# The last two expert places combined on TensorE, and the context branch moved into the expert stage

## The chip, the cores and the metric

The kernel runs on one core of a Trainium2 chip. The metric is the device time of one execution in microseconds (us), the median of several runs. Places in the trace are given in us from the start of the span.

## The reference, cut to what matters

Two transformer blocks follow one another on 512 tokens of 1024 numbers, all in fp32. The first block ends in a mixture of experts: each token goes to 2 of 32 experts. The second block takes the normed sum, and also a second, short sequence, the context (256 tokens), of which only one small state is needed.

```python
# first block, after its mixer (TOP_K = 2, N_EXPERTS = 32)
def expert_block(args):
    xb, e = args
    hid = jax.nn.silu(xb @ w_gate[e]) * (xb @ w_up[e])
    return hid @ w_down[e]
y = jnp.sum(y_buf[dest].reshape(T, TOP_K, D) * weights[..., None], axis=1)
x = x + y
# second block
h_lat = _rms_norm(x, norm_mix) * (1.0 + sc1) + sh1
h_ctx = _rms_norm(ctx, norm_mix) * (1.0 + csc1) + csh1
... = jnp.split(h_lat @ w_in, ...)
... k_c, v_c, ..., gf_c, gb_c = jnp.split(h_ctx @ w_in, ...)
s_f = _gla_final_state(kh_c, vh_c, lgf_c)                # k, v and log gates of the context
s_b = _gla_final_state(_rev(kh_c), _rev(vh_c), _rev(lgb_c))
o_l = _gla_bidir(qh_l, kh_l, vh_l, lgf_l, lgb_l, s_f, s_b)   # starts from these two states
```

`_log_gate` is a product with a narrow matrix, a second one, and a log-sigmoid; `_gla_final_state` sums k, times an exponential of a running sum of the log gates, times v.

## The kernel before, in words

**Expert stage.** The rows of the 512 tokens are sorted by expert into 34 slots of 64 rows. The kernel visits them as 32 "places": places 1 to 24 have one slot of 64 rows, 25 and 26 have two (128 rows), 27 to 32 one. A place loads 12 chunks of 512 KB of its expert's weights (eight for up and gate, four for down) and multiplies each in plain fp32, two products of 512 columns (`products` in `expert_block`). SyncE (SP) issues all chunk loads in order into a ring of tiles called "raw"; the ring has 25 tiles (`wraw`, `mr`, `nr`, `whi`, `wlo`, `xr`), 19 after place 13. A load waits until TensorE is done with the tile's last user. The order of TensorE's instructions is written by hand: `ORDER = "uuutssgududssududu"` says, for each place, when an up/gate chunk of this place (u), a transposition or down chunk of the place before (t, d), a step of gathering rows for a later place (g) or a step of side work (s) comes. The side work from place 13 on is `spectrum` (filters of the second block); in place 31 it is `context_hidden`.

**What a place leaves.** y of a place (64 x 1024) goes from PSUM by a DVE copy (L891) and an ACT copy to a tile, and by a DMA to a buffer in HBM (`ybuf`, `g.Y`). So y of place k is copied while place k+1 runs. Beside the 34 slots `ybuf` has 15 blocks for a rare overflow; they are filled with zeros early on (`zz`). A loop `For_i` after the last place handles overflow blocks; with this input it runs no time, but its bound is loaded from SBUF into each engine's registers, and the engines pass its branch.

**After the last place.** `context` runs on TensorE (with weights split into two fp32r halves and three products for one, `dense_nat`), while POOL issues eight indirect gathers `yk<-ybuf` (128 rows of 4 KB each, L971). On DVE eight scalar-tensor-tensor operations (L977) add them, weighted, to the residual x, which was loaded again from HBM after the last chunk (`load_x`, L247). Then come squares, a square root by eleven small DVE operations (`rsqrt`), the scaled rows `xn`, and `mixer2` transposes them (`hidden_T`, L1237) and starts its big products.

Of the kernel before, what the change touches and what calls it, by code (L numbers as in the profile page):

```python
# [24 lines left out]
SPEC = 13  # L25


ORDER = "uuutssgududssududu"

# [220 lines left out]
def mixer1(g, mp):  # L250
# [95 lines left out]
    for kt in range(8):  # L346
# [311 lines left out]
def routing(g, first):  # L658
# [131 lines left out]
    g.sloti = g.b2c.tile([128, 2, 4], I32, name="sloti")  # L790
    V.tensor_copy(g.sloti, g.slot)
# [59 lines left out]
def expert_block(g, pool, x, e, store, queue=None):  # L851


    nc, A = g.nc, g.A
    n = x.shape[2]
    w = A["l_moe"][e] if isinstance(e, int) else A["l_moe"][ds(e, 1)].rearrange("o p a c -> (o p) a c")
# [8 lines left out]
    def products(ps, lhs, c, first, last):  # L865
        raw = ring(g, "raw", [128, 2, 512], F32)
        nc.sync.dma_start(raw.rearrange("p a b -> p (a b)"), w[:, c, :])
        for i in range(2):
            nc.tensor.matmul(ps[i], lhs, raw[:, i, :], start=first, stop=last)  # L869
# [20 lines left out]
    y = g.yg.tile([128, 1024], F32, name="y", tag="y", bufs=2)[0:n]  # L890
    nc.vector.tensor_copy(y[:, 0:512], pd[0])  # L891
    nc.scalar.activation(y[:, 512:1024], pd[1], AF.Copy)  # L892
    (queue or nc.gpsimd).dma_start(store, y)
# [3 lines left out]
def moe(g, pool, xg):  # L897
# [8 lines left out]
    place, last, side = 0, None, iter(())  # L906
    with g.tc.manual_schedule(engines={mybir.EngineType.PE}):
        for i, (b0, nb, double) in enumerate(groups):
            steps, nxt = rows(i + 1) if i + 1 < len(groups) else (iter(()), None)
            if i == 7:  # L910
                context_norm(g, pool)
            next(steps, None)
            for b in range(0, nb, 2 if double else 1):
                e = place
                if place >= DBL:
                    e = nc.values_load(g.eoi[0:1, 32 + place:33 + place], engines=[eng], min_val=0, max_val=31)
                place += 1
                r0, n = (b0 + b) * 64, 128 if double else 64
                block = expert_block(g, pool, xg[0][:, :, b * 64:b * 64 + n], e, g.Y[r0:r0 + n, :],
                                     queue=nc.scalar if place == 32 else None)  # L920
                if place == SPEC:

                    g.rings["raw"] = [r for r in g.rings["raw"] if r[0] is not g.resid and r[1] != "nr"]
# [1041 lines left out]
```

## Time and profile before

| | us |
|---|---|
| Median of 3 runs (lowest, highest) | 1560.48 (1560.05, 1561.49) |
| Profiled execution, whole | 1556.2 |
| Its span, first to last instruction | 1554.2 |
| TensorE (PE) busy in it | 1457.9 (94 %) |
| VectorE (DVE) busy | 797.5 (51 %) |
| ScalarE (ACT) busy | 525.9 (34 %) |
| GpSimd (POOL) busy | 128.2 (8 %) |
| First and last y copy of the expert stage (L891) | 370.5, 864.8 |
| Mean granted TensorE clock | 0.976 |

A busy PE is one with a product in flight, which can still be slow or wait for its weights; so the stage has to be read by what PE waits for and by the distance of the y copies. The profiled execution took 4.3 us less than the median of the runs; sums are made within it.

### The profile page before, as it was taken

How to read it: one execution, taken by the hardware profiler on the slowest of the kernel's cores; microseconds unless marked ns; L12 is line 12 of the kernel's file. 1: busy time of each engine (PE TensorE's matmuls, PEld its weight loads, DVE VectorE, ACT ScalarE, POOL GpSimd, SP SyncE). 2: the span in 40 equal slices, each digit the busy share in tenths (PEclk: the TensorE clock that was granted, in tenths of full speed). 3: DMA queues.
4: the chain of work that ended last, by engine and by line, in shares of the span. 5: the costliest groups of instructions: out<-in, count | busy, mean ns of one | idle time of the engine just before them, and what ended most of it. 6: DMA issues, size and time to landing. Idle time of an engine off the chain costs nothing. (4 is left out here: it accounts for less than half of the span.)

```text
span 1554.2 us, 19403 instructions
## 1 busy us (share of the span) xinstructions
PE 1457.9 (94%) x7024; PEld 989.4 (64%) x7024; DVE 797.5 (51%) x1496; ACT 525.9 (34%) x859; POOL 128.2 (8%) x119
## 2 busy tenths in 40 slices
PE   7999999959999889899999689999999999999997
PEld 6776777844443234444444458887787888888886
DVE  6888858681111340312202494789868652344344
ACT  5444545321111242421112353333435442134331
POOL 1111000030000010110100220000301000000010
PEclk9999999979999999899999799999999999999999
DMA  8442261768999999999999835336522522222321
GB/s 282 128 156 89 87 185 54 241 258 329 410 410 410 381 409 411 381 368 409 373 385 410 309 119 163 97 109 202 162 97 98 200 88 89 95 95 96 101 89 55
DMA packets 123450, 343.10 MB, mean 221 GB/s; under 512 B 11823, under 2 KB 14866, under 8 KB 123352
## 3 DMA queue, kind: packets, MB, share of 16 engines
q1 hardware_dynamic: 115576, 320.15, 57.2%
q0 software_dynamic: 5248, 17.10, 2.8%
q10 hardware_dynamic: 2528, 4.59, 1.0%
q8 instruction: 56, 0.92, 0.3%
q14 instruction: 42, 0.34, 0.1%
HBM read 322.69 MB, written 19.14 MB: 220 GB/s over the span
## 5 line engine op out<-in xcount | busy, mean ns | idle before, releaser
L151 DVE TENSOR_TENSOR wlo<-wraw,whi 128x1024 fp32r<-128x1024 f32 (+2 forms) x136 | 163.9, 1205 | 207.2 <-ACT whi L150 206.2
L150 ACT ACTIVATE whi<-wraw 128x1024 fp32r<-128x1024 f32 (+1 forms) x142 | 146.9, 1034 | 341.3 <-PE acc L157 189.8
L891 DVE COPY y<-acc 64x512 f32<-64x512 f32 (+1 forms) x32 | 21.8, 682 | 234.2 <-PE acc L869 234.2
L869 PE MATMUL acc<-mr,xg 128*64 128x512 f32 (+1 forms) x488 | 127.5, 600 | 4.8 <-DMA mr<-in_l_moe 4.7
L156 PE MATMUL acc<-h3hi,whi 128*128 128x512 f32 (+1 forms) x272 | 102.8, 379 | 1.1 <-ACT h3hi L1263 1.1
L157 PE MATMUL acc<-h3hi,wlo 128*128 128x512 f32 (+1 forms) x272 | 102.4, 377 | 0.0
L158 PE MATMUL acc<-h3lo,whi 128*128 128x512 f32 (+1 forms) x272 | 102.0, 378 | 0.1
L158 PE MATMUL acc<-wlo,mh 128*128 128x512 f32 x224 | 88.8, 397 | 0.0
L157 PE MATMUL acc<-whi,ml 128*128 128x512 f32 x224 | 88.7, 396 | 0.0
L156 PE MATMUL acc<-whi,mh 128*128 128x512 f32 x224 | 88.7, 396 | 0.0
L892 ACT ACTIVATE y<-acc 64x512 f32<-64x512 f32 (+1 forms) x32 | 19.0, 593 | 192.4 <-DVE y L891 170.9
L869 PEld LDWEIGHTS acc<-mr,xg 128*64 128x64 f32 (+1 forms) x488 | 34.9, 139 | 77.2 <-issue 53.0
L1046 DVE SCALAR_TENSOR_TENSOR adac<-wraw,sc,adac 128x512 f32<-128x512 f32 x100 | 80.3, 810 | 6.6 <-POOL adac L1042 3.2
L869 PE MATMUL acc<-wraw,xg 128*64 128x512 f32 (+1 forms) x276 | 71.6, 602 | 1.8 <-DMA wraw<-in_l_moe 1.8
L156 PE MATMUL acc<-whi,xh 128*128 128x512 f32 x160 | 64.4, 402 | 8.3 <-ACT whi L150 8.3
L869 PE MATMUL acc<-mr,hT 128*64 128x512 f32 (+1 forms) x252 | 69.8, 597 | 1.1 <-DMA mr<-in_l_moe 1.1
L157 PE MATMUL acc<-whi,xl 128*128 128x512 f32 x160 | 64.0, 400 | 0.0
L158 PE MATMUL acc<-wlo,xh 128*128 128x512 f32 x160 | 63.8, 401 | 0.0
L156 PEld LDWEIGHTS acc<-h3hi,whi 128*128 128x128 f32 x272 | 51.2, 188 | 10.5 <-ACT h3hi L1263 1.3
L846 PE MATMUL pgx<-G,hh 128*128 128x256 f32 (+1 forms) x288 | 53.7, 311 | 4.5 <-DVE G L827 4.5
L158 PEld LDWEIGHTS acc<-h3lo,whi 128*128 128x128 f32 x272 | 50.9, 188 | 9.7 <-DVE h3lo L1265 0.3
L157 PEld LDWEIGHTS acc<-h3hi,wlo 128*128 128x128 f32 x272 | 51.2, 188 | 9.2
(704 smaller groups left out, 2987.8 us busy)
## 6 DMA issues: line engine op xcount, KB each, us to landing
mr<-in_l_moe SPq DMA_DIRECT2D x185, 512.0 KB, 10.7
wraw<-in_l_moe SPq DMA_DIRECT2D x94, 512.0 KB, 10.1
wraw<-in_w_mlp SPq DMA_DIRECT2D x64, 512.0 KB, 3.9
wraw<-in_w_in SPq DMA_DIRECT2D x56, 512.0 KB, 4.0
wraw<-in_w_ada SPq DMA_DIRECT2D x48, 512.0 KB, 3.7
whi<-in_l_moe SPq DMA_DIRECT2D x36, 512.0 KB, 10.3
wlo<-in_l_moe SPq DMA_DIRECT2D x35, 512.0 KB, 10.2
xr<-in_l_moe SPq DMA_DIRECT2D x20, 512.0 KB, 10.7
```

What stands on the lines that cost most here:

```text
L150: nc.scalar.activation(hi[:, :nk, :ncol], raw[:, :nk, :ncol], AF.Copy)
L151: eng.tensor_tensor(lo[:, :nk, :ncol], raw[:, :nk, :ncol], hi[:, :nk, :ncol], op=OP.subtract)
L156: g.nc.tensor.matmul(ps, ah, bh, start=start, stop=False)
L157: g.nc.tensor.matmul(ps, al, bh, start=False, stop=False)
L158: g.nc.tensor.matmul(ps, ah, bl, start=False, stop=stop)
L846: nc.tensor.matmul(pg[:, :n], src[:, tt, ks], G[:, tt, :n], start=i + tt == 0, stop=i == 1 and tt == 3)
L869: nc.tensor.matmul(ps[i], lhs, raw[:, i, :], start=first, stop=last)
L891: nc.vector.tensor_copy(y[:, 0:512], pd[0])
L892: nc.scalar.activation(y[:, 512:1024], pd[1], AF.Copy)
L1046: nc.vector.scalar_tensor_tensor(acc[v], raw[:, k, :], s, acc[v], op0=OP.mult, op1=OP.add)
```

## The change

1. The zero fill of `ybuf` goes, and `ybuf` has only the first 32 slots.
2. The context branch is made inside the expert stage: its norm beside place 5, the rest as side work of places 9 to 12, as plain fp32 products from weights loaded into six tiles of the ring. Its state is copied to `S0` there. `context_hidden` in place 31 and `context` after the loop go.
3. The residual x is loaded again before place 31's chunks, no longer after the last chunk.
4. Places 31 and 32 keep their y in SBUF (a `spare` tile) and follow an order of their own, `LAST`. A one-hot matrix times the weights (`slot_weights`) is made as side work in place 31.
5. After place 30 the eight gathers are issued, into ring tiles, and eight DVE operations (L1047) add them to x.
6. After the loop `add_rows` adds places 31 and 32: eight fp32 products of 128 x 128 by 512 columns, and eight DVE additions from PSUM. Squares are on ACT, and there are two root chains (three rows of tiles, then one).
7. An overflow block would add to x in the loop itself.

```diff
-SPEC = 13
+SPEC, CTX = 13, 2
+LAST = "uuutsuddddssuuuu"
...
-    zz = mp.tile([64, 1024], F32, name="zz", tag="p", bufs=4)
-    nc.gpsimd.memset(zz, 0.0)
-    nc.sync.dma_start(g.Y[64 * NST:64 * (NST + NMAX), :].rearrange("(b p) c -> p b c", p=64),
-                      zz[:, None, :].to_broadcast([64, NMAX, 1024]))
...
-            if i == 7:
+            if i == CTX - 1:
                 context_norm(g, pool)
+            if i == CTX:
+                side = context(g, pool)
...
-                if place == 31:
-                    for _ in side:
-                        pass
-                    side = context_hidden(g, pool)
...
+        load_x(g, g.xs)
+        spare = [g.moe.tile([128, 2, 512], F32, name="spare", tag="nr", bufs=g.nn) for _ in range(2)]
+        keep = spare[0].rearrange("p a b -> p (a b)")
+        side = last_slots(g, pool, groups[-1][0], spare[1])
+        for b in range(2):
+            block = expert_block(g, pool, xg[0][:, :, b * 64:b * 64 + 64], chunks(), keep[b * 64:b * 64 + 64], keep=True)
+            run(LAST, block)
+            if b == 0:
+                gathered(g)
...
-    load_x(g, g.xs)
-
-    context_load(g)
...
+    more_blocks(g, pool, nmore)
+    add_rows(g, keep, g.wl)
+    squares(g)
...
+def gathered(g):
     nc = g.nc
+    y = {}
     for tt in range(4):
         for k in range(2):
+            y[tt, k] = ring(g, "raw", [128, 2, 512], F32).rearrange("p a b -> p (a b)")
+            nc.gpsimd.indirect_dma_start(out=y[tt, k], out_offset=None, in_=g.Y,
                                          in_offset=bass.IndirectOffsetOnAxis(ap=g.sloti[:, k, tt:tt + 1], axis=0))
+    for tt in range(4):
+        for k in range(2):
+            x = g.x[:, tt, :]
+            nc.vector.scalar_tensor_tensor(x, y[tt, k], g.wy[:, k, tt:tt + 1], x, op0=OP.mult, op1=OP.add)
+
+
+def add_rows(g, y, w):
+
+    for tt in range(4):
+        for h in (slice(0, 512), slice(512, 1024)):
+            ps = g.ps.tile([128, 512], F32, name="pc", tag="acc" if h.start else "t", bufs=4)
+            g.nc.tensor.matmul(ps, w[:, tt * 128:tt * 128 + 128], y[:, h], start=True, stop=True)
+            x = g.x[:, tt, h]
+            g.nc.vector.tensor_tensor(x, x, ps, op=OP.add)
...
+    def half(c0, out):
+
+        ps = g.ps.tile([128, 2, 256], F32, name="pkv", tag="t", bufs=4)
+        raw = []
+        for c in (0, 4):
+            raw.append(ring(g, "raw", [128, 2, 512], F32).rearrange("p a b -> p (a b)").rearrange("p (a b) -> p a b", a=4))
+            nc.sync.dma_start(raw[-1], A["w_in_2"][0][c * 128:c * 128 + 512, c0:c0 + 256].rearrange("(a p) c -> p a c", p=128))
+        for tt in range(2):
+            for k in range(8):
+                nc.tensor.matmul(ps[:, tt], h[:, k, tt * 128:tt * 128 + 128], raw[k // 4][:, k % 4], start=k == 0, stop=k == 7)
+            if tt == 0:
+                yield
+        nc.scalar.activation(out, ps, AF.Copy)
         yield
```

TensorE in the middle of places 9 to 12, as it stands now (L879 is a chunk's product, L891 the transpositions of gu, L1439 the context's narrow product, L1398 the gates, L1456 its k and v):

```order
L879 MATMUL acc<-whi,hT 64x512 x2
L1439 MATMUL pgr<-hc,wg2f 32x256 x8
L1398 MATMUL pz<-gk,gr 128x512 x2
L879 MATMUL acc<-xr,xg 64x512 x2
...
L891 MATMUL pth<-identf,gu 128x64 x4
L1456 MATMUL pkv<-mr,hc 128x256 x16
L840 MATMUL pgx<-G,hh 128x256 x4
...
L879 MATMUL acc<-mr,hT 64x512 x2
L1456 MATMUL pkv<-mr,hc 128x256 x16
L879 MATMUL acc<-mr,xg 64x512 x2
```

The context's products stand between chunk products, where before only chunk products stood.

SP at the end of the chunk loads, as it stands now with its waits (L855 is a chunk load; the last five are the last up/gate chunk and the four down chunks of place 32; `DMASW` are the gathers, `PE` and `DVE` the tile's last user):

```order
L855 DMA mr_6607<-in_l_moe 128x1024 [waits DMAHW2_49,PE_49]
L855 ISA
L855 DMA whi_6611<-in_l_moe 128x1024 [waits DMAHW3_49,DMASW5_49,DVE_49]
...
L855 DMA wlo_6627<-in_l_moe 128x1024 [waits DMAHW4_49,DMASW6_49,DVE_49]
...
L855 DMA wraw_6639<-in_l_moe 128x1024 [waits DMAHW7_49,DMASW1_49,DVE_49]
L139 DMA wraw_7073<-in_w_in_2 128x2x512 [waits DMAHW0_49,DMASW2_49,DVE_49]
...
L1134 DMA wraw_7114<-in_w_ada_2 128x2x512 [waits DMAHW3_49,PE_49]
L989 COMPARE_AND_BRANCH
```

The last five chunks now wait for a gather and for the DVE addition that reads it; four loads for `mixer2` stand ahead of the loop's branch.

DVE at the end of the stage, before (L891 y copy, L877 gate times up, L977 the additions of gathered rows, L1365 the context's k times its exponential):

```order
L891 COPY y<-acc 64x512
L877 TENSOR_TENSOR gu<-acc,gu 64x512
L891 COPY y<-acc 64x512
L151 TENSOR_TENSOR wlo<-wraw,whi 128x2x256
L948 TENSOR_LOAD eoi
...
L977 SCALAR_TENSOR_TENSOR xb<-yk,wk,xb 128x1024 x2
L1365 TENSOR_TENSOR kw<-s4c,kn 128x2x4x64
L977 SCALAR_TENSOR_TENSOR xb<-yk,wk,xb 128x1024
L1365 TENSOR_TENSOR kw<-s4c,kn 128x2x4x64
L980 SCALAR_TENSOR_TENSOR yk,css<-xa 128x1024 x2
```

and now (L901 y copy, L887 gate times up, L1047 the additions of gathered rows, L1057 those from `add_rows`):

```order
L901 COPY y<-acc 64x512
L887 TENSOR_TENSOR gu<-acc,gu 64x512
L1047 SCALAR_TENSOR_TENSOR xa<-whi,wy,xa 128x1024
...
L1047 SCALAR_TENSOR_TENSOR xb<-wraw,wy,xb 128x1024 x4
L901 COPY spare<-acc 64x512
L887 TENSOR_TENSOR gu<-acc,gu 64x512
L901 COPY spare<-acc 64x512
L941 TENSOR_LOAD eoi
...
L1057 TENSOR_TENSOR xa<-xa,pc 128x512 x4
L1057 TENSOR_TENSOR xb<-xb,pc 128x512 x4
L66 TENSOR_SCALAR sq<-sq 128x3
```

The eight additions of gathered rows moved from behind the loop to ahead of place 31's y copy and place 32's gate-times-up; behind the loop stand eight additions from PSUM and the root chains.

## Rows read from the trace of the kernel before

**Rows 1.** The page's first and second parts: PE's total; GB/s in 40 slices.

```profile
PE 1457.9 (94%) x7024; PEld 989.4 (64%) x7024; DVE 797.5 (51%) x1496; ACT 525.9 (34%) x859; POOL 128.2 (8%) x119
...
GB/s 282 128 156 89 87 185 54 241 258 329 410 410 410 381 409 411 381 368 409 373 385 410 309 119 163 97 109 202 162 97 98 200 88 89 95 95 96 101 89 55
```

**Rows 2.** Line L891, the y copies: duration min/median/max in ns, first and last start.

```profile
L891 DVE COPY y<-acc x32: 675/683/692, 370.5 to 864.8; 64x512 f32<-64x512 f32 x30, 128x512 f32<-128x512 f32 x2
```

**Rows 3.** DVE's timeline: the y copies of places 8, 12 and 17.

```profile
460.84 0.68 DVE L891 COPY y<-acc 64x512 f32<-64x512 f32 x1 [10.35 <-PE acc L869]
...
526.52 0.68 DVE L891 COPY y<-acc 64x512 f32<-64x512 f32 x1 [0.52 <-PE acc L869]
...
615.74 0.68 DVE L891 COPY y<-acc 64x512 f32<-64x512 f32 x1 [17.58 <-PE acc L869]
```

**Rows 4.** PE's weight loads, waits in 526 to 616: us, times, longest.

```profile
PEld acc L869 <- DMA mr<-in_l_moe: 6.5, 10, 1.8
PEld acc L869 <- DMA whi<-in_l_moe: 2.8, 3, 1.1
PEld acc L869 <- DMA wraw<-in_l_moe: 1.5, 4, 0.5
...
PEld acc L869 <- DMA wlo<-in_l_moe: 1.1, 1, 1.1
```

**Rows 5.** PE's waits in 616 to 847.

```profile
PE pth L881 <- DVE gu L877: 10.6, 3, 6.3
```

**Rows 6.** Stages: busy us per engine (instructions), granted clock, DMA share, GB/s.

```profile
800.00:860.00 60.00, 57.24 (x302) 23.83 (x298) 11.72 (x22) 13.10 (x31) 2.66 (x5) 1.00 1.03 411
...
860.00:870.00 10.00, 4.12 (x20) 1.39 (x20) 1.43 (x3) 1.60 (x3) 0.00 (x0) 0.97 0.85 293
870.00:880.00 10.00, 8.92 (x28) 6.16 (x29) 2.93 (x4) 5.77 (x7) 6.30 (x7) 0.52 0.71 257
880.00:890.00 10.00, 4.99 (x22) 4.29 (x21) 7.92 (x9) 4.11 (x5) 2.80 (x3) 0.66 0.95 373
```

**Rows 7.** DMA issues in 400 to 860: KB each, median us to landing.

```profile
mr<-in_l_moe SPq DMA_DIRECT2D x156, 512.0 KB, 10.7
...
ybuf<-y POOLq DMA_DIRECT2D x26, 256.0 KB, 5.9
...
xc<-in_ctx SPq DMA_DIRECT2D x1, 1024.0 KB, 11.4
...
xa<-xs SPq DMA_DIRECT2D x2, 512.0 KB, 10.8
```

**Rows 8.** Timelines of PE and SP: fp32 products; the last chunk loads.

```profile
470.10 1.03 PE L869 MATMUL acc<-mr,xg 128*64 128x512 f32 x4
470.96 1.03 PE L869 MATMUL acc<-mr,hT 128*64 128x512 f32 x4
...
926.20 3.70 PE L1292 MATMUL pz<-gk,gr 33*128 33x512 f32 x8
...
847.87 2.34 SPq L867 DMA_DIRECT2D wraw<-in_l_moe  x2
```

**Rows 9.** Timeline of 860 to 914, the steps named in the text.

```profile
862.82 1.89 PE L869 MATMUL acc<-wraw,hT 128*64 128x512 f32 x8
...
864.75 0.68 DVE L891 COPY y<-acc 64x512 f32<-64x512 f32 x1 [4.69 <-PE acc L869]
...
871.08 0.58 PE L156 MATMUL acc<-whi,hch 128*128 128x256 f32 x1 [6.38 <-SPq L951]
...
871.87 1.08 POOL L971 DMA_INDIRECT yk<-ybuf,sloti  x1 [12.20 <-ACT whi L150]
...
878.46 1.28 DVE L977 SCALAR_TENSOR_TENSOR xa<-yk,wk,xa 128x1024 f32<-128x1024 f32 x1 [3.43 <-DMA yk<-ybuf,sloti]
...
911.54 1.11 DVE L987 TENSOR_SCALAR xn<-xb,hl_y 128x1024 f32<-128x1024 f32 x1
...
912.58 0.67 DVE L1401 COPY S<-pS 128x512 f32<-128x512 f32 x1
```

More of the change, by code (lines that the diff above doesn't have):

```diff
@@ L848, in gather, with __init__, load, take @@
         yield
-def expert_block(g, pool, x, e, store, queue=None):
-    nc, A = g.nc, g.A
+class Chunks:
+    def __init__(self, g, e):
+        w = g.A["l_moe"]
+        self.g, self.raw = g, {}
+        self.w = w[e] if isinstance(e, int) else w[ds(e, 1)].rearrange("o p a c -> (o p) a c")
+    def load(self, c):
+        self.raw[c] = raw = ring(self.g, "raw", [128, 2, 512], F32)
+        self.g.nc.sync.dma_start(raw.rearrange("p a b -> p (a b)"), self.w[:, c, :])
+    def take(self, c):
+        if c not in self.raw:
+            self.load(c)
+        return self.raw.pop(c)
+def expert_block(g, pool, x, chunks, store, keep=False):
+    nc = g.nc
     n = x.shape[2]
-    w = A["l_moe"][e] if isinstance(e, int) else A["l_moe"][ds(e, 1)].rearrange("o p a c -> (o p) a c")
     def pair():
@@ L865, in products @@
     def products(ps, lhs, c, first, last):
-        raw = ring(g, "raw", [128, 2, 512], F32)
-        nc.sync.dma_start(raw.rearrange("p a b -> p (a b)"), w[:, c, :])
+        raw = chunks.take(c)
         for i in range(2):
@@ L906, in moe, with chunks, run @@
     place, last, side = 0, None, iter(())
+    def chunks():
+        nonlocal place
+        e = place
+        if place >= DBL:
+            e = nc.values_load(g.eoi[0:1, 32 + place:33 + place], engines=[eng], min_val=0, max_val=31)
+        place += 1
+        return Chunks(g, e)
+    def run(order, block, ngather=0):
+        nonlocal last
+        for which in order:
+            if which == "u":
+                next(block)
+            elif which == "s":
+                next(side, None)
+            elif which == "g":
+                for _ in range(ngather):
+                    next(steps, None)
+            elif last:
+                next(last)
+        last = block
@@ L939, in moe @@
-                last = block
-            xg = nxt
+                run(ORDER, block, 8 * (2 if double else 1) // nb)
+            xg = nxt
+        for _ in side:
+            pass
+        load_x(g, g.xs)
[7 more added lines that the diff above has]
+                gathered(g)
@@ L991, in combine @@
+        if tt == 1:
+            nc.scalar.activation(row, x, AF.Copy, scale=g.rx[tt])
+        else:
+            g.last = nc.vector.tensor_scalar(row, x, g.rx[tt], None, op0=OP.mult).ins
+        rows.append(row)
     return rows
@@ L1339, in context @@
+    kn = ring(g, "raw", [128, 2, 512], F32)[:, :, 0:256]
+    yield from half(1792, kn)
+    vn = ring(g, "raw", [128, 2, 512], F32)
+    yield from half(2048, vn[:, :, 0:256])
     for tt in range(2):
```

203 lines of the change are left out of this document (110 added, 93 removed).

## Prediction

> **What bounds the kernel now.** The page comes first: PE is busy for 94 % of the span, and the 40 slices show a plateau near 410 GB/s from slice 11 on [rows 1]. The reader should take the two together: through the expert stage either PE or the chunk stream sets the pace, and the share alone doesn't say which. The y copies do. The first lies at 370.5 [rows 2], place 8's at 460.84 [rows 3]; 90.3 us for seven places is 12.9 a place, PE's own pace (a chunk's product takes 0.86, from one start to the next [rows 8], and twelve of them with transpositions and row gathering fill the 12.9). A place also needs 12 chunks, 6.29 MB, which is 15.3 us at 411 GB/s [rows 6]. So PE first eats a lead of loaded chunks and then, from place 9 on, waits for chunks: places 9 to 12 take 65.7 us (to 526.52), places 13 to 17, with the filters beside them, 89.2 (to 615.74) [rows 3]. In that stretch PE's weight loads wait 6.5 + 2.8 + 1.5 + 1.1 = 11.9 us for chunks [rows 4]. After it PE waits for no chunk; what is left is 10.6 us for gate-times-up behind ACT and DVE [rows 5]. Late PE then holds the ring's tiles, and the stream is PE's follower until about 800. From 800 to 860 it is at 411 GB/s again [rows 6], and the last places use up the lead.
>
> The stage ends with the last product at 862.82 + 1.89 = 864.7; call that P. Then nothing big is on PE that the second block waits for: the last normed row is done at 911.54 + 1.11 = 912.65 [rows 9], which is P + 47.9. In between lie the write of y, the loop's branch (PE resumes at 871.08, P + 6.4), eight gathers from 871.87, eight additions from 878.46, squares, root and scaling [rows 9].
>
> **The change part by part.**
>
> *Zero fill.* It was a write off every engine's path, long before the expert stage; PE is covered there by its own dense products. I take nothing for it; if that cover were gone, it would be worth the transfer, 3.9 MB at 411 GB/s, 9.6 us, as a gain.
>
> *Context in places 9 to 12, on PE.* Weights of 64 columns cost 0.43 per product of 512 (0.86 for a chunk's two [rows 8]). With 128 columns four products of 512 take 3.70 [rows 8], 0.92 each, so 0.46 for 256 columns. The 48 products for k and v are then 22.1 us at most; by the step of 0.43 (twice that of 64 columns) 20.6. The narrow product has 32 columns, 8 x 0.21 = 1.7; two gate products 1.9; six of 256 columns 2.6; eight of 128 columns and sixteen transpositions about 4. Sum 31. The gate's chain on ACT can also hold up gate-times-up; one such wait is up to 6.3 [rows 5], nothing at best; I take 4. At PE's pace place 12's y then comes at 460.84 + 4 x 12.9 + 35 = 547.4, 21 us later than now.
>
> *The same on the DMA engines.* Six loads of 512 KB, 3.15 MB, in runs of 1 KB. The nearest row on such runs is 860 to 870, where the context's weights were loaded before: 293 GB/s at a share of 0.85, 345 at full share [rows 6]; that is 9.1 us (7.7 at 411). The context itself, 1 MB, moves from a place where PE set the pace to one where the stream does [rows 7]: 2.6. So the chunks come 11.7 later. The Trainium skill ("DMA: Bandwidth & Descriptors", Specifications) has line rate from 512 B upward, which would make the 9.1 a 7.7; this trace's stretch with the 1 KB runs is slower than its chunk stretches, and no row separates the runs from what else moved there.
>
> *What is left at place 17.* PE is 21 late at place 12 and can recover the 11.9 of chunk waits in places 13 to 17: 9 left. The stream is 11.7 late and PE can't pass it. I take S = 12; bounds: 1 (also the 10.6 of rows 5 recovered) and 21 (nothing recovered). Later PE waits for no chunk, so S is carried to 800.
>
> *Places 31 and 32: what is new in the stream.* x again, four loads of 512 KB [rows 7], 2.10 MB, now ahead of place 31's chunks instead of behind the last; eight gathers of 512 KB, 4.19 MB, ahead of the last five chunks; one y write of 0.26 MB less. 6.03 MB at 411 GB/s [rows 6] are 14.7 us on the last landing. By the Trainium skill (same page and section, an HBM limit of 358 GB/s per core) it would be 16.8; the trace's 411 is the measured rate here, and I use that. There was slack: the last chunk's load is the second of two from 847.87, which ends at 850.21, so it was issued at 849.9, and the median of 10.7 to landing [rows 7, 8] gives 860.6; its product began about 0.86 before 864.7, at 863.9. So 3.3 are absorbed, and P moves by 11.4 more. `context_hidden` leaves place 31, which only makes PE wait longer there: nothing. Does the gather chain hold the last chunks or place 32's gate-times-up longer? From place 30's y: write 5.9 [rows 7], eight gathers 1.4 apart (1.08 busy and a gap), 6.6 from a first gather to a first addition [rows 9], 1.3 for the last: 25 us. The stream, with 6 MB more, needs about as long for the 12 + 4 chunks after that y. I take nothing beyond 11.4; bound +6 (each step at the 10.7 of a loaded queue).
>
> *After P.* No y is written at the end, but the next weights' loads and the eviction are on the way, so the branch is passed about as before, P + 6.4 [rows 9]. The eight products of 512 columns with 128-column weights cost 0.92 each at full clock, 7.4, and twice that at half. The granted clock was 0.97 in 860 to 870, 0.52 in 870 to 880, after PE had stood from 864.7 to 871 [rows 6, 9]: near 1.2 GHz for about ten us after PE resumed. So I take the products as two thirds at half clock: 11 to 12 us, to P + 18. Behind them: one addition 0.9, one square 1.2, a chain of eleven operations of 0.2, with two scalings of 1.1 and another chain's tail between them on DVE, and the last scaling 1.1: 8 us. Last row at P + 26 instead of P + 47.9: 21.9 gained. The wait of 8 us on PE before `hidden_T` is new in its length; before, the context's small products stood there. A wait of that size cost the clock in 880 to 890 (0.66, with PE at work for 4.99 [rows 6]), so I charge 3 us. The Trainium skill ("TensorE: Matmul & The Clock Gate", HAM oscillation) says that waits between bursts bring the array back to its low clock; these rows agree. Bounds of the tail's gain: 15 (all at half) to 25 (full clock throughout). The copy of S on DVE, 0.67 [rows 9], goes too.
>
> *Other edits.* The bound's early load and the loop's own addition cost nothing with no overflow; the slot weights' few DVE and PE operations lie beside chunk products.
>
> *Sum.* 12 + 11.4 - 18.9 - 0.7 = +3.8, made in the profiled execution of 1556.2 (span 1554.2), which stands 4.3 under the median of the runs. On the median of 1560.5 it gives 1564.3; slightly over what a measurement here can tell from no change, 0.2 % or 3.1 us.
>
> **The rivals.**
>
> *PE swallows the context (faster).* If besides the 11.9 of chunk waits the 10.6 behind gate-times-up also shrink, and the stream's lateness goes into the lead that it has from place 17 on, S is 1 to 3: 2 + 11.4 - 18.9 - 0.7 = -6.2, 1554. For it: after 616 no chunk is waited for [rows 5], so the stream has slack. Against: a wait for DVE in one's own place isn't filled by being late. It decides at S below 5. Chance 0.29.
>
> *The clock stays up after P (no change).* If PE passes the loop in 4 us, before the clock falls, the products take 7.4: rows 6 us sooner, at P + 20: -2.2, 1558. For it: no y write is waited for at the loop. Against: PE's next work is still behind a branch and a load. Chance 0.20.
>
> *Nothing is recovered (clearly slower).* PE's places 13 to 17 are filled by the filters, the stream is late as well, so waits stay and S is 20; or the gathers' additions keep the last five chunks back by 6 to 8. Either gives +11 to +13: 1572 to 1573. For it: on SP and on DVE the last chunks and gate-times-up are queued behind eight additions. Chance 0.18.
>
> **How the numbers follow.** The forecast of +3.8 (its own range 1562 to 1569) has 0.33. Faster by over 0.2 %: the first rival, 0.29. Within 0.2 %: the second, 0.20. Slower: forecast and third, 0.51. The range 1552 to 1576 takes in both outer rivals with the bounds of S and of the tail, leaving out less than 2 in 10.
>
> **What would show it.** Place 12's y near 547 and place 17's near 628; the same distance up to place 29. The last product near 888, and a last landing 26 later than now. The last normed row 26 after the last product, the clock near half in the additions. Wrong would be: a place 17 less than 5 or more than 18 late; a y of place 30 or eighth addition that PE waits for at the end; rows ready earlier than P + 21 or later than P + 32; a first product of the second block that waits for weights, since it starts sooner and its splits have less time.

## The result, and the profile after

| | before | after |
|---|---|---|
| Median of 4 runs each (us) | 1560.99 | 1576.18 |
| Lowest, highest | 1560.05, 1563.19 | 1573.87, 1578.34 |
| Ratio, 95 % interval | | 1.0094 [1.0078, 1.0109] |
| Span of the profiled execution | 1554.18 | 1572.06 |

The kernel became slower, by some 14.7 us. The forecast was slower too, but by 3.8; the median of 1576.18 stands 0.2 above the upper end of the range of 1552 to 1576, and 1.0094 times the 1560.5 that the forecast was made on is 1575.2, just inside it. The y copies show where the 17.9 us of the two spans lie. First the source line of the copies after the change (duration, first and last start), to be read beside [rows 2]; the copies of places 31 and 32 now go to other tiles (`spare`).

```profile
L901 DVE COPY y<-acc x30: 675/683/692, 371.1 to 868.1; 64x512 f32<-64x512 f32 x28, 128x512 f32<-128x512 f32 x2
```

Then the timeline of after (start, duration, engine, line; in brackets how long the engine stood before it, and for what): the y copies of places 8, 12, 17, 29 and 30, and what follows up to the last normed row.

```profile
469.41 0.68 DVE L901 COPY y<-acc 64x512 f32<-64x512 f32 x1 [2.27 <-PE acc L879]
...
555.29 0.68 DVE L901 COPY y<-acc 64x512 f32<-64x512 f32 x1 [0.18 <-PE acc L879]
...
643.14 0.68 DVE L901 COPY y<-acc 64x512 f32<-64x512 f32 x1 [19.21 <-PE acc L879]
...
856.95 0.68 DVE L901 COPY y<-acc 64x512 f32<-64x512 f32 x1 [10.21 <-PE acc L879]
...
868.05 0.68 DVE L901 COPY y<-acc 64x512 f32<-64x512 f32 x1 [8.55 <-PE acc L879]
...
876.61 1.04 POOL L1042 DMA_INDIRECT whi<-ybuf,sloti  x1 [6.37 <-DMA mr<-in_l_moe]
...
884.24 1.28 DVE L1047 SCALAR_TENSOR_TENSOR xa<-whi,wy,xa 128x1024 f32<-128x1024 f32 x1 [9.77 <-DMA whi<-ybuf,sloti]
...
901.96 1.28 DVE L1047 SCALAR_TENSOR_TENSOR xb<-wraw,wy,xb 128x1024 f32<-128x1024 f32 x1 [1.35 <-DMA wraw<-ybuf,sloti]
...
903.16 0.68 DVE L901 COPY spare<-acc 64x512 f32<-64x512 f32 x1
...
904.99 0.68 DVE L887 TENSOR_TENSOR gu<-acc,gu 64x512 f32<-64x512 f32 x1 [1.15 <-ACT gu L886]
...
911.56 1.02 PE L879 MATMUL acc<-wraw,hT 128*64 128x512 f32 x4
...
914.68 7.13 PE L1055 MATMUL pc<-spare 128*128 128x512 f32 x16 [2.10 <-ACTq L989]
...
928.71 0.75 DVE L1095 TENSOR_SCALAR xn<-xb,sq 128x1024 f32<-128x1024 f32 x1
```

The last scaling of a row ends at 928.71 + 0.75 = 929.46, 16.8 after the last y copy began (912.63). In one table, with the steps' terms beside what they measured in the two profiled executions (before from [rows 2, 3, 9] and the copies of places 7 and 29 at 447.9 and 829.3):

| stretch | before | after | difference | predicted |
|---|---|---|---|---|
| up to place 7's y | 447.9 | 448.6 | +0.6 | 0 |
| place 7's y to place 17's | 167.8 | 194.6 | +26.8 | S = 12 |
| place 17's y to place 29's | 213.6 | 213.8 | +0.2 | 0 |
| place 29's y to the last y copy | 35.4 | 55.7 | +20.3 | 11.4 |
| last y copy to last normed row | 47.9 | 16.8 | -31.1 | -19.6 |
| behind it | 641.5 | 642.6 | +1.1 | (in the line above) |

All three terms have the right sign, and all three are too small; the two costs came out 23.7 higher, the gain of the tail, with what lies behind it, 10.4. That the whole still ended near the range is luck: two errors of opposite sign took away part of each other.

**Where PE and the stream stand.** Windows of after (PE, PEld, DVE, ACT, POOL busy, with instructions; granted clock; DMA share; GB/s), against [rows 6]:

```profile
470.00:480.00 10.00, 8.35 (x42) 5.61 (x39) 2.08 (x4) 3.99 (x6) 0.54 (x1) 1.00 0.35 89
...
500.00:510.00 10.00, 10.00 (x56) 5.90 (x52) 1.98 (x3) 3.41 (x6) 0.34 (x1) 1.00 0.35 90
...
540.00:550.00 10.00, 7.04 (x35) 3.33 (x33) 0.00 (x0) 4.94 (x7) 0.00 (x0) 0.83 0.99 360
...
555.00:643.00 88.00, 82.23 (x384) 33.02 (x384) 29.12 (x47) 27.93 (x48) 11.86 (x14) 1.00 1.03 410
...
880.00:890.00 10.00, 5.80 (x20) 1.09 (x20) 3.24 (x3) 0.00 (x0) 4.85 (x6) 0.85 1.03 410
890.00:900.00 10.00, 5.35 (x12) 0.59 (x8) 5.14 (x5) 0.00 (x0) 0.00 (x0) 0.50 1.03 409
...
910.00:920.00 10.00, 7.90 (x23) 2.96 (x20) 4.12 (x6) 3.66 (x5) 0.00 (x0) 0.95 0.20 57
920.00:930.00 10.00, 4.98 (x20) 3.42 (x19) 9.04 (x30) 3.74 (x7) 2.72 (x4) 0.73 0.00 0
```

Three things are to be seen. While the context runs (460 to 550) the stream stops in the middle of its plateau, at 89 and 90 GB/s, and PE stays busy for 8.35 to 10 of ten beside these stops; only in 540 to 550 is it down to 7.04, at a granted clock of 0.83. From 555 to 643, places 13 to 17, the stream is at 410 again, and these five places take 87.8 us, against 89.2 before. And at 880 to 900 the stream is saturated and PE is not: 5.8 and 5.35 busy in ten, with the granted clock going from 0.85 to 0.50, the lower of its two levels (1.2 GHz).

What SP waits for in 430 to 550 after the change (us, times, longest), and below it SP's own timeline there:

```profile
SPq L855 <- DVE xr L1480: 14.4, 1, 14.4
SPq L855 <- PE acc L879: 13.5, 8, 5.2
```

```profile
464.81 2.19 SPq L1215 DMA_DIRECT2D fsm<-in_c_filt  x1
478.66 0.36 SPq L855 DMA_DIRECT2D mr<-in_l_moe  x1
```

So there are two long kinds of stop, beside shorter waits for tiles that PE still uses (13.5 in eight pieces). Between 467.00 and 478.66 SP issues nothing and waits for nothing: in the order of its instructions 19 loads of an expert's number into a register, each with two further instructions, stand between these two rows, 0.61 each. The 14.4 are the wait for a ring tile that still holds the context's k, until line 1480 has multiplied it.

The weight loads' waits in places 13 to 17 (556 to 643), which answer to [rows 4], and PE's own waits there:

```profile
PEld acc L879 <- DMA mr<-in_l_moe: 6.1, 8, 1.1
PEld acc L879 <- DMA wraw<-in_l_moe: 3.5, 4, 1.1
PEld acc L879 <- DMA wlo<-in_l_moe: 2.9, 3, 1.1
PEld acc L879 <- DMA whi<-in_l_moe: 2.3, 3, 1.1
```

```profile
PE pth L891 <- DVE gu L887: 3.5, 3, 2.4
PE acc L879 <- DMA mr<-in_l_moe: 1.0, 5, 0.2
PE acc L879 <- DMA wraw<-in_l_moe: 0.6, 3, 0.2
PE acc L879 <- DMA wlo<-in_l_moe: 0.4, 2, 0.2
PE acc L879 <- DMA whi<-in_l_moe: 0.2, 1, 0.2
```

PE's own waits for chunks in the same places before (526 to 616):

```profile
PE acc L869 <- DMA mr<-in_l_moe: 1.5, 4, 0.9
PE acc L869 <- DMA whi<-in_l_moe: 0.4, 2, 0.2
PE acc L869 <- DMA wlo<-in_l_moe: 0.2, 1, 0.2
```

So PE itself stood 2.1 for chunks in these places before the change, and 2.2 after it.

PE's waits at the end, 855 to 930:

```profile
PE pth L891 <- DVE gu L887: 9.2, 1, 9.2
PE acc L879 <- DMA mr<-in_l_moe: 7.3, 14, 1.5
PE pt L1343 <- DVE xn L1095: 5.0, 1, 5.0
```

### The profile page after: what moved, and what is told of

The parts are those of the page before. It is cut to its first block, busy times and chain, and to the rows that moved or that the text cites. A ratio compares the mean times of both kernels' runs of the same rounds, so it can differ in the third digit from the quotient of the medians.

```text
span 1572.1 us, 19410 instructions
## 1 busy us (share of the span) xinstructions
PE 1471.5 (94%) x7036; PEld 993.8 (63%) x7036; DVE 788.1 (50%) x1507; ACT 527.2 (34%) x858; POOL 115.0 (7%) x113
## 3 DMA queue, kind: packets, MB, share of 16 engines
q1 hardware_dynamic: 115736, 316.35, 55.5%
## 5 line engine op out<-in xcount | busy, mean ns | idle before, releaser
L153 DVE TENSOR_TENSOR wlo<-wraw,whi 128x1024 fp32r<-128x1024 f32 (+1 forms) x132 | 161.2, 1221 | 201.7 <-ACT whi L152 201.3
L152 ACT ACTIVATE whi<-wraw 128x1024 fp32r<-128x1024 f32 (+1 forms) x134 | 140.1, 1046 | 326.3 <-PE acc L159 187.2
L879 PE MATMUL acc<-mr,xg 128*64 128x512 f32 (+1 forms) x496 | 135.3, 611 | 5.9 <-DMA mr<-in_l_moe 5.9
L901 DVE COPY y<-acc 64x512 f32<-64x512 f32 (+1 forms) x30 | 20.5, 682 | 239.3 <-PE acc L879 239.3
L879 PEld LDWEIGHTS acc<-mr,xg 128*64 128x64 f32 (+1 forms) x496 | 36.7, 142 | 80.7 <-issue 54.2
L879 PE MATMUL acc<-mr,hT 128*64 128x512 f32 (+1 forms) x248 | 66.7, 596 | 2.9 <-DMA mr<-in_l_moe 2.4
L879 PE MATMUL acc<-wraw,xg 128*64 128x512 f32 (+1 forms) x260 | 67.8, 603 | 0.9 <-DMA wraw<-in_l_moe 0.8
```

What stands on the lines that cost most here:

```text
L152: nc.scalar.activation(hi[:, :nk, :ncol], raw[:, :nk, :ncol], AF.Copy)
L153: eng.tensor_tensor(lo[:, :nk, :ncol], raw[:, :nk, :ncol], hi[:, :nk, :ncol], op=OP.subtract)
```

## The experiments

The theories at the start: (A) the stops of the stream cost the 27 us in places 9 to 17, and the queues' order and held tiles make them; (B) PE is simply full with the context's products, and the stops hide behind it; (C) the end's 20 us are the gathers' additions, which stand on DVE's in-order queue ahead of place 31's last copies; (D) they are the bytes of x and of the gathers. All kernels compute the whole reference. "Start" is place 7's y against before's 447.9; it comes from ahead of the stretches that are read (the granted clock differs there from one execution to the next: in 50 to 100 it is 1.00 in before and 0.93 in kernel 4; the second kernel is short of loaded chunks from place 6 on, where its y copies come 16 apart), so stretches are compared. The stretches are of one profiled execution each: kernels 4, 6 and 7 change nothing up to place 17, and theirs from place 7's y to place 17's lie between 194.1 and 195.4.

| kernel | start | y7 to y17 | y29 to last y | last y to last row | ratio, 95 % |
|---|---|---|---|---|---|
| before | 0 | 167.8 | 35.4 | 47.9 | 1 |
| after | +0.6 | 194.6 | 55.7 | 16.8 | 1.0094 [1.0078, 1.0109] |
| 1 context only | +0.2 | 195.4 | 34.7 | 39.2 | 1.0106 [1.0061, 1.0150] |
| 2 SP in program order | +6.9 | 196.4 | 55.2 | 16.9 | 1.0158 [1.0120, 1.0196] |
| 3 k, v off the ring | +5.0 | 195.7 | 56.1 | 16.9 | 1.0123 [1.0091, 1.0155] |
| 4 gathers to own tiles | +6.0 | 195.3 | 54.5 | 18.6 | 1.0108 [1.0071, 1.0146] |
| 5 v first | +2.4 | 191.9 | 55.5 | 16.9 | 1.0104 [1.0075, 1.0133] |
| 6 additions late | 0 | 195.4 | 47.8 | 22.3 | 1.0080 [1.0053, 1.0106] |
| 7 x early | +5.4 | 194.1 | 49.5 | 16.9 | 1.0069 [1.0046, 1.0091] |
| 8 = 5 + 6 + 7 | +4.2 | 192.7 | 41.8 | 24.1 | 1.0052 [1.0037, 1.0066] |
| 9 none held | +4.0 | 189.7 | 56.0 | 18.5 | 1.0079 [1.0057, 1.0101] |
| 10 = 9 + 6 + 7 | +2.6 | 189.7 | 42.1 | 24.6 | 1.0039 [1.0021, 1.0057] |
| 11 combination only | +4.4 | 166.1 | 56.0 | 39.1 | 1.0066 [1.0052, 1.0080] |
| 12 = 11 + x early | +5.5 | 166.7 | 49.3 | 37.7 | 1.0029 [1.0016, 1.0042] |

**1. The context alone.** The kernel before, with the context's part of the change and the rest of it undone:

```diff
-            if i == 7:
+            if i == CTX - 1:
                 context_norm(g, pool)
+            if i == CTX:
+                side = context(g, pool)
...
-    context_load(g)
...
-    context(g, pool)
```

> The kernel before with one part of the change: the context branch in places 9 to 12 and its norm beside place 5. Gathers, additions and y writes stay as they were, behind the loop. The profile of the changed kernel has place 17's y 27.4 us later than before. Theory (the stream of chunks is held up in places 9 to 12): place 17's y 26 to 28 late here too, and place 29's as well; behind the last product the gathers and the row chain still take most of their 47.9, since the context was hidden behind them, so the last normed row comes 40 to 45 after the last product and the whole is slower by 18 to 24, 1579 to 1585. Rival (what was lost comes from the gathers at the end, and the context costs only the 12 us of the forecast): place 17's y 12 late, the whole slower by at most 8.

The last y copy on DVE's timeline, and the last scaling of a row, which is on ACT's:

```profile
891.83 0.68 DVE L891 COPY y<-acc 64x512 f32<-64x512 f32 x1 [6.45 <-PE acc L869]
...
929.88 1.14 ACT L989 ACTIVATE xn<-xb,hl_y 128x1024 f32<-128x1024 f32 x1
```

The context costs the same 27.6 in places 8 to 17 as in after, and nothing at the end of the stage. It gives 8.7 back behind the last product, far less than the whole change does. Place 17 came as the theory had it; the row came a little earlier than its 40 to 45 (39.2), and the whole, 1577.3, stayed just under its 1579 to 1585. The two parts of the change can be read apart up to the last product; behind it they can't.

**2 to 4. One suspect each.** The second kernel puts SP's queue in program order, which spreads the register loads; the third takes k and v off the ring; the fourth gives the gathers tiles of their own and frees the ring for the last chunks.

```diff
-    with g.tc.manual_schedule(engines={mybir.EngineType.PE}):
+    with g.tc.manual_schedule(engines={mybir.EngineType.PE, mybir.EngineType.SP}):
```

> The changed kernel with SyncE's instructions in the order of the program, so that the 22 loads of expert numbers into SyncE's registers, which stand behind the load of the filter constants at 465 to 478, stand each ahead of its own place again. Theory (the register loads stop the stream): the stretch 470 to 480 rises from 89 GB/s to about 400. If nothing else held the stream, place 17's y would come 10 to 12 earlier; but the tile that keeps the context's k is a tile of the ring and holds SyncE until k has been used, near 507, so I expect only 2 to 6 of it, 1570 to 1574. Rival (PE's own work sets places 9 to 17, the stream's gaps are harmless): place 17's y unchanged within 1, the whole unchanged within 3.

```diff
             if i == CTX:
+                g.rings["raw"] = [r for r in g.rings["raw"] if r[1] != "nr"]
...
-    kn = ring(g, "raw", [128, 2, 512], F32)[:, :, 0:256]
+    kn = t[:, 0, :, 0:256]
...
-    vn = ring(g, "raw", [128, 2, 512], F32)
+    vn = g.moe.tile([128, 2, 512], F32, name="vn", tag="nr", bufs=g.nn)
```

> The changed kernel with the context's k, v and weighted k in tiles of their own (the ring has 23 tiles instead of 25 from place 9 on; k lies in the dead half of the gates' tile, so the exponentials come one step earlier). Theory (a ring tile that holds k blocks SyncE for 14.4 us): the stretch 500 to 510 rises from 90 GB/s to over 350, place 17's y comes 6 to 12 earlier, the whole 1564 to 1570. Rival (PE sets the pace): place 17's y unchanged within 1, 1576 within 3. Two tiles less in the ring could take back some of it.

```diff
-            y[tt, k] = ring(g, "raw", [128, 2, 512], F32).rearrange("p a b -> p (a b)")
+    t = [xtile(g, [128, 2, 2, 512], "yx", F32) for _ in range(2)]
...
+        add_gathered(g)
```

> The changed kernel with the eight gathers of rows in tiles that the ring doesn't use, so that the last five chunk loads wait for no gather and no addition. DVE still has seven of the eight additions ahead of place 31's y copy and of place 32's gate times up. Theory (DVE's order holds the end: PE waits 9.2 for that product): the chunks land earlier but gate times up doesn't come earlier, since the additions still wait for gathers that share the DMA engines with the chunks; the distance from place 29's y to the last product stays within 3 of 55.7, the whole 1573 to 1577. Rival (SyncE's waits for gathers hold the last chunks): that distance falls by 6 to 10, 1566 to 1570.

The second and the third didn't bring what (A) had expected: their wholes are 1583.9 and 1578.9, and place 17 isn't earlier in either, although the stretches at 470 (390 GB/s) and at 500 (392 GB/s) did rise. The fourth's own theory held, 54.5 within 3 of 55.7, with the whole at 1578.7. SP's longest waits in 430 to 560, first of the second kernel, then of the third:

```profile
SPq L855 <- DVE xr L1480: 19.8, 1, 19.8
```

```profile
SPq L1190 <- PE acc L879: 10.8, 1, 10.8
```

The stop only moved: with the register loads out of the way the wait for k's tile grew from 14.4 to 19.8, and with k off the ring SP waited for a tile that PE held. The distance from place 7's y to place 17's stayed at 195.3 to 196.4 in all. The second kernel's late start, +6.9, is a cost of its own order. The fourth shows that freeing the ring is worth 1.2 at the end (54.5 against 55.7), so tiles are a small part of what (C) explains.

**5. v before k, and SP in program order only from the context on,** so that k's tile is never held for v:

```diff
-    kn = ring(g, "raw", [128, 2, 512], F32)[:, :, 0:256]
-    yield from half(1792, kn)
...
+    yield from half(2048, lambda ps: evict("vn", ps))
+    yield from half(2304, lambda ps: evict("vn", ps, slice(256, 512)))
+    yield from half(1792, lambda ps: evict("kw", ps))
```

> The changed kernel with two of the stream's stops taken away at once: from place 9 on SyncE keeps the order of the program (register loads each ahead of its place, except five that stay together), and the context makes v first and k last, straight from PSUM, so that no ring tile holds k, and the one with v is held for less than a turn of the ring. TensorE's products are the same. Theory (a stream that is stopped in places 9 to 12 has no lead to give back, so PE's loss is kept): from place 7's y to place 17's y it took 167.8 before and 194.5 to 196.4 in all the kernels with the context there; with 10 or more of the lost 23 us of stream back, it falls to 183 to 189, the whole 1566 to 1572. Rival (PE's added work and nothing else): 194 to 197 again, the whole 1574 to 1580.

A window of this kernel:

```profile
510.00:520.00 10.00, 9.80 (x52) 6.31 (x50) 0.16 (x1) 0.77 (x2) 0.00 (x0) 1.00 0.07 28
```

The stream stopped once more, at another place (28 GB/s), because v's tile is now the one that is held; PE was busy for 9.8 of these 10 all the same. 191.9 is 2.7 better, about twice what executions differ by; it lies between the theory's 183 to 189 and the rival's 194 to 197, and the whole, 1576.5, is the rival's.

**6. The additions behind place 32's gate-times-up,** with the gathers in their own tiles:

```diff
-    nc.vector.tensor_tensor(h, up, a, op=OP.mult)
+    g.gu = nc.vector.tensor_tensor(h, up, a, op=OP.mult).ins
...
+        with g.tc.issue_after(g.gu):
+            add_gathered(g)
```

> The changed kernel with the gathered rows in tiles of their own and all eight additions behind place 32's gate times up on DVE. Theory (that order on DVE is what held the last place: PE waited 9.2 for it): from place 29's y to the last y 55.7 in the changed kernel falls to 44 to 48; the additions, ten us of them, now end some 5 after the last product, so 2 to 5 of it are given back behind it; the whole 1568 to 1573. Rival (6 MB more on the DMA engines hold the last chunks, whatever DVE's order): 53 to 56 again, the whole 1574 to 1578.

PE's wait for `gu` at the end (840 to 930) and its wait behind the last product, then the two ends on the timeline:

```profile
PE pth L891 <- DVE gu L887: 1.4, 1, 1.4
PE pc L1062 <- SPq L991: 5.7, 1, 5.7
```

```profile
904.64 0.68 DVE L901 COPY spare<-acc 64x512 f32<-64x512 f32 x1 [1.99 <-PE acc L879]
...
926.16 0.75 DVE L1102 TENSOR_SCALAR xn<-xb,sq 128x1024 f32<-128x1024 f32 x1
```

The 9.2 fell to 1.4 and the last copy came 7.9 sooner: (C) is right for this part, and the whole, 1570.9, is in the theory's range. Kernel 4, which differs from this one only by where the additions stand, puts 1.2 of the 7.9 down to the tiles and 6.7 to the order on DVE. Of the 7.9, 5.4 went back behind the last product (22.3 against 16.8): PE stands 5.7 there instead of 2.1, for the loop's branch, and `add_rows`' products take 8.93 instead of 7.13, at a granted clock of 0.80 in 910 to 920. The last addition now ends at 909.16, and PE resumes at 910.34; that the branch waited for the additions is likely, but not shown.

**7. x loaded ahead of place 27's chunks,** where the stream still has slack:

```diff
+            if i == 7:
+                for _ in side:
+                    pass
+                load_x(g, g.xs)
...
-        load_x(g, g.xs)
```

> The changed kernel with x loaded again ahead of place 27 instead of place 31, in the stretch where the stream waits for PE and not PE for the stream. Theory (the end is bound by the 6 MB that were added to it): 2.1 MB less there are 5.1 us; from place 29's y to the last y 55.7 falls to 50 to 52, the whole 1569 to 1573. Rival (the end is bound by the chain place 30's y, write, gathers, additions, gate times up, and not by the chunks): within 2 of 55.7, the whole 1574 to 1578.

49.5 instead of 55.7, with nothing lost behind, and 1571.1 for the whole, as the theory had it: 6.2, near the 5.1 that 2.10 MB are worth at 411 GB/s. (D) is right for this part.

**8. The three together** (5, 6 and 7).

> The three edits together: v first and SyncE in program order, gathered rows in own tiles with the additions behind place 32's gate times up, x loaded ahead of place 27. Theory: the gains add up, 8 at places 9 to 17 and 14 at the end, less 4 given back behind the last product: 1555 to 1563, at or below the kernel before. Rival (PE's added work is kept and the end stays with its bytes): 1568 to 1575.

The gains of 6 and 7 add up: 41.8. Place 17's y gains 1.9 and not the 8 that were hoped for, and the whole, 1568.3, is in the rival's range.

**9. No tile held at all,** after 5: k and v in tiles that leave the ring at the context's start, and the other tiles that leave it go earlier, at place 11.

```diff
             if i == CTX:
+                shrink(g, lambda r: r[1] != "nr")
                 side = context(g, pool)
...
+                if place == 11:
+                    shrink(g, lambda r: r[0] is not g.resid)
...
-            kv[name] = ring(g, "raw", [128, 2, 512], F32)
+            kv[name] = g.moe.tile([128, 2, 512], F32, name=name, tag="nr", bufs=g.nn)
```

> The changed kernel with nothing left that stops SyncE ahead of its turn in places 9 to 13: v and the weighted k in two tiles taken out of the ring at place 9, v first and k last, program order on SyncE from place 9, the four tiles of the residual taken out of the ring at place 11 instead of 13, and the ring turned so that the next load after each cut goes to its oldest tile. The ring is smaller (23, then 19 tiles). In the kernel with v first the stream was stopped for 15.3 us at a tile that waited for the state's product, lost its whole lead there, and places 12 to 17 took as long as ever. Theory (a stop at a held tile drains the lead, a ring that is only full does not): the lead stays 20 us or more through place 13, and from place 7's y to place 17's y it takes 180 to 188 instead of 192 to 196; the whole 1562 to 1570. Rival (places 13 to 17 take 88 us whatever the lead, because the filters fill PE there): 192 to 196 again and 1572 to 1578; then places 13 to 17 would show no chunk waits and a lead of over 20 us.

This is the run that decides between (A) and (B). PE's waits from 528 to 642 (places 11 to 17), all that there are:

```profile
PE pth L897 <- DVE gu L893: 5.5, 4, 2.9
```

and its windows, two in the context and one over places 13 to 17:

```profile
470.00:480.00 10.00, 8.35 (x42) 3.80 (x39) 3.10 (x4) 7.49 (x9) 0.54 (x1) 1.00 1.04 390
...
500.00:510.00 10.00, 9.40 (x47) 5.82 (x44) 1.36 (x2) 3.45 (x5) 0.54 (x1) 1.00 0.38 112
...
555.00:641.00 86.00, 80.48 (x382) 35.25 (x380) 29.15 (x47) 27.94 (x48) 11.76 (x14) 0.98 1.03 410
```

The stop at 470 is gone (390 GB/s instead of 89). The stream still falls once, to 112 GB/s in 500 to 510, where SP waits for tiles that PE still uses (8.4 for one with the context's weights), but PE waits for no chunk any more from place 7's y on; and still 189.7 of the 194.6 remain. From place 7's y to place 12's PE is busy for 99.5 us and waits 3.6 for other engines, the whole 103.1; in places 13 to 17 it is busy for 80.5 and waits 5.5 for `gu`, the whole 86. So the stops cost 4.9 us, and the rest of the 26.8, 21.9, is (B). The 189.7 lies between theory and rival; the whole, 1574.0, and the missing chunk waits are the rival's.

**10. The same with 6 and 7.**

> The same with the two edits at the end: gathered rows in tiles of their own with the additions behind place 32's gate times up, and x loaded ahead of place 27. Those two gave about 12 us from place 29's y to the last y, less 1 to 5 behind it. Theory: 1550 to 1560, below the kernel before. Rival (places 13 to 17 as long as ever): 1565 to 1570, as the kernel with all three earlier edits.

The product of the last chunk, on PE's timeline:

```profile
895.84 1.15 PE L885 MATMUL acc<-mr,hT 128*64 128x512 f32 x4 [0.26 <-DMA mr<-in_l_moe]
```

At the end 42.1, which leaves 6.7 over before, and the last product waits for its chunk to land. The gathers' 4.19 MB are 10.2 at 411 GB/s, minus the 3.3 of slack 6.9. So the rest fits (D) again; no kernel was run without the gathers. The whole, 1568.0, is the rival's.

**11 and 12. The combination alone,** with the context where it was; then with x early as well.

```diff
-            if i == CTX - 1:
+            if i == 7:
                 context_norm(g, pool)
-            if i == CTX:
-                side = context(g, pool)
...
+    context_load(g)
     more_blocks(g, pool, nmore)
...
+    context(g, pool)
```

> The other part of the change alone: places 31 and 32 combined from the SBUF by TensorE, the gathers beside them, x loaded ahead of place 31, no zero fill; the context as in the kernel before (half of it as side work in place 31, the rest behind the loop, split into fp32r halves). Place 17's and 29's y stand where they stood in the kernel before, within 1 to 5 (the start of the stage differs by that much from run to run). The end costs about 20 as in the changed kernel: last y 54 to 57 behind place 29's, some 3 to 5 more with the context's side work there. Theory (the context's products were hidden behind the gathers before; with rows that are ready 17 after the last product there is nothing to hide them behind): the rows come 17 to 26 after the last product and the context's 20 us of products are paid in part, the whole within 6 of the kernel before, 1557 to 1567. Rival (DVE and PE have room for the context under the second block's first steps): 1546 to 1553, faster by as much as the tail gained.

> The same with x loaded ahead of place 27. Theory (2.1 MB in a stretch in which the stream waits for PE are 3 to 5 us less at the end, as with the context in places 9 to 12): 3 to 5 less than the combination alone, 1553 to 1563. Rival (the end is held by the chain of gathers and additions ahead of place 32's gate times up): the same as the combination alone.

Kernel 11's timeline, from the last y copy to the last scalings of rows, with one POOL operation that is named below:

```profile
888.96 0.68 DVE L902 COPY spare<-acc 64x512 f32<-64x512 f32 x1 [7.38 <-PE acc L880]
...
917.31 2.51 POOL L154 TENSOR_TENSOR wlo<-wraw,whi 128x1024 fp32r<-128x1024 f32 x1 [0.30 <-ACT whi L153]
...
917.48 2.89 DVE L1094 TENSOR_SCALAR xn<-xa,sq 128x1024 f32<-128x1024 f32 x1
...
925.70 1.42 DVE L1094 TENSOR_SCALAR xn<-xb,sq 128x1024 f32<-128x1024 f32 x2 [5.33 <-PE acc L161]
...
926.97 1.14 ACT L1092 ACTIVATE xn<-xa,sq 128x1024 f32<-128x1024 f32 x1
```

Without the context in places 9 to 12 the distance to place 17 is that of before (166.1), and the end costs its 20.5 as in after. Behind the last product the combination alone gains 8.8 and not 31: the context's work on PE, DVE and ACT stands between the rows now (two scalings wait 5.33 for a product of the context). So the row comes 39.1 and not 17 to 26 after the last product, and the whole, 1571.3, lies above both ranges, 1557 to 1567 and 1546 to 1553. Twelve gains 6.7 at the end, more than its 3 to 5; its whole, 1564.9, is still above 1553 to 1563. It has the lowest ratio of all these kernels (the interval of kernel 10 overlaps it), and is still 0.29 % slower than before.

## Why the prediction was off

**Bounds of the stage.** That PE eats a lead and then waits for chunks was right for places 9 to 12. For places 13 to 17 the reading of [rows 4] was wrong, and it is the step that failed: "PE is 21 late at place 12 and can recover the 11.9 of chunk waits in places 13 to 17: 9 left." Weight loads run beside products. A wait on PEld is PE's time only where the product before it has ended. Before the change the weight loads wait 11.9 for chunks there and PE itself 2.1; after it the weight loads wait 14.8 (6.1 + 3.5 + 2.9 + 2.3), and PE itself 2.2. With PE waiting for no chunk at all (kernel 9) the five places take 86.4 against 89.2 before. So 2.8 was to be had, not 11.9; after got 1.4. One view would have shown it: PE's own waits, and PE's busy time plus those, against the length of the stretch.

**Place 12.** Its y was to come 21 us later and came 28.1 later, counted from place 7's. In kernel 9, where PE waits for hardly anything, it is 24.6: places 8 to 12 take 103.2, 38.7 over the 64.5 of PE's own pace, against the 35 that were worked out from fp32 products. So 3.6 of the 7.1 missing are work that was undersized. The other 3.5 are the stops (PE's own waits for chunks from 460 to 556 are 3.2 in after, none in kernel 9), which the prediction had only as bytes ("the chunks come 11.7 later") and not as a queue that issues nothing: before, the 28 register loads are spread from 348.1 to 828.4, after the change the last stands at 477.9. S is then 21 + 3.6 + 3.5 - 1.4 = 26.7; 26.8 was measured.

**The stream's bytes** in places 9 to 12 set nothing: in kernel 9, which loads the same bytes there, no chunk is waited for.

**The end.** "I take nothing beyond 11.4" failed by a term that the third rival had priced: the additions keep "the last five chunks back by 6 to 8". It measured 7.9 (kernel 6), but by another way than those words: 6.7 of it is the order on DVE, ahead of `gu` (which the rival names in what speaks for it), and only 1.2 the chunks' tiles (kernel 4). The chain is seen in the timeline of after: place 30's y 868.05, the first gather issued at 876.61, the first addition at 884.24, and then additions about 2.5 apart, since each waits for a gather that shares a saturated stream (409 GB/s). On DVE's queue they stand ahead of place 31's copy, which ran at 903.16 (in kernel 6, where they stand behind it, at 885.12), and of `gu`, at 904.99; PE stood 9.2. The prediction estimated the chain at 25 and the stream "about as long" (16 chunks and the gathers, 12.6 MB, are 30.6 at 411 GB/s); the chain took 35.2 (868.05 to 901.96 + 1.28 = 903.24). Of the 10 more, 2.7 lie before the first gather (8.6 against 5.9; POOL waited 6.4 there, by the profile for the landing of a chunk), 1.0 before the first addition, and 6.5 in the seven steps between the additions (17.7, where eight of 1.4 had been taken). Bytes: x 6.2 (kernel 7), gathers 6.7 (kernel 10), 12.9 together, near the 11.4. Sum 20.8; measured 20.3. A part of these terms is clock, which no run sets apart: the granted clock stands at 0.50 in 890 to 910, and the products of the last four chunks take 5.6 (906.94 to 912.58), against 3.7 before.

**Behind the last product.** The sign and the parts were right, the time before PE resumes was not. Predicted was P + 6.4, as in [rows 9], and a clock that has fallen. PE's rows began 2.1 after the last product, with no y write waited for at the loop, and the granted clock was 0.95 in 910 to 920. The eight products (sixteen records) took 7.13 (predicted 7.4 at full clock, 11 to 12 as taken), and what follows 7.65 (predicted 8). That is the second rival's mechanism, at P + 16.9 instead of its P + 20 (P is 912.58 now). The half clock before `hidden_T` came (0.73 in 920 to 930, after a wait of 5.0), but all that lies behind the last row costs 1.1, not 3. The Trainium skill ("TensorE: Matmul & The Clock Gate", HAM oscillation) puts such a fall down to waits between bursts; the 0.50 of 890 to 900, a stretch in which PE waited for chunks and for `gu`, agrees. Beside the stand of 2.1 behind the last product the clock was 0.95, beside the 5.7 of kernel 6 it was 0.80.

**The rivals** weren't alternatives. The third came true in both its halves (the second by DVE's order and hardly by the chunks), the second as well, and they act on different stretches, so that their sizes add. By its own terms the third stands at +9.8 to +11.8, not +11 to +13. The forecast took each term near its middle, and both costs ended beyond their upper bounds (21 for S, 17 for the end), as the tail's gain did beyond its own (25). Three of the prediction's own signs of being wrong came: place 17 more than 18 late, an eighth addition ahead of a `gu` that PE waits for, and rows earlier than P + 21.

**The two parts don't add up either.** Context alone costs 16.5 (1.06 % of 1561), the combination alone 10.3, both 14.7 and not 26.8. The tail accounts for it: -8.7 and -8.8 alone, -31.1 together, since the rows are only early when neither a write with gathers nor the context's products stand between. The context is thus the price of the early rows: 27 on a full PE for some 22 more behind the stage. The combination's 20 before the stage's end are the rest.

**Zero fill:** no run tells it apart; up to place 7's y the two profiled executions differ by 0.6.

**Open:** what the 4.9 of kernel 9 are made of (all held tiles and the register loads were taken away at once there; one at a time the stops only moved), and why x is worth 6.2 and not the 5.1 of its bytes. Kernel 11's scaling took 2.89 instead of 0.75 beside a POOL operation, and ended 0.55 after it; the context's second k-times-exponential there took 2.73 beside another one (914.60 to 917.01) and again ended 0.55 after it, where the first, with POOL idle, took 0.69. Kernel 12's trace repeats both. So DVE seems to have waited for POOL; no run takes POOL's part away, and the last row didn't wait for it.

## What to carry to other kernels

Work put "beside" an engine is free only as far as that engine was held up there: the context added 38.7 us to PE's own pace in places 8 to 12 (kernel 9), 14.0 of it went into time that these places lost before the change as well, 2.8 came back in places 13 to 17, and the other 21.9 were paid. Before a wait is counted as room, ask whether the engine itself stood still in it, for a wait of the weight loads that lies under the product before is no room. On engines and queues that work in order, ask of each new instruction that may wait what stands right behind it; eight short additions cost 6.7 us by where they stood (7.9 with their tiles), and another place for them was worth 2.4 in the sum, since PE then stood longer behind the last product. And a part of a change can be worth nothing without the other, so the parts are to be tried one by one and together.

## What was not expected of the hardware

Nineteen small register loads on SP, 0.61 us each, stopped a stream of 410 GB/s for 11.7 us; PE, which had a lead, waited only 3.2 for chunks up to place 12's y. A stop that one change took away showed up at the next instruction in the queue that could wait: 14.4 became 19.8 on the same tile. Additions that each wait for a gather beside a saturated stream (409 GB/s) start 2.5 us apart, though POOL issues the gathers 1.3 apart. And two DVE operations that ran beside a POOL operation took 2.73 and 2.89 instead of 0.69 and 0.75.
